# GLA's values as seven products of half sums, with the four GLA heads spread over three gated units

## The chip, the core and the metric

The kernel runs on one core of a Trainium2 chip. A core has a matrix engine (PE, TensorE; PEld is its weight load), VectorE (DVE), ScalarE (ACT), GpSimd (POOL), and SyncE (SP), whose queue issues most DMAs; POOL's queue issues others, among them DMAs that add to what lies at their destination. Each engine works off its own instructions in a fixed order and waits on semaphores. The metric is device time in microseconds; less is better.

## What is computed

One layer of a hybrid encoder: 512 tokens of width 2048, float32.

```python
mod = silu(c) @ w_cond + b_cond
shift, scale, gate = split(mod, 3)
h = rms_norm(x) * (1 + scale) + shift
aq, ak, av, ag, gq, gk, gv, gg, lr_f, lr_b = split(h @ w_in)
# attention, 16 heads x 64: three dilated windows merged by their denominators
a_out = att * silu(ag)
# GLA, 4 heads, dk 128, dv 256: gated linear attention, forward and backward
log_g = log_sigmoid(lr @ gate_up + bias) / 16
g_out = rms_norm(o_fwd + o_bwd) * gla_norm_gain * silu(gg)
y = concat(a_out, g_out) @ w_out
out = rms_norm(x + gate * y) * final_gain
```

The change concerns `gv = h @ w_in[:, 5120:6144]`: 512 x 2048 by 2048 x 1024.

## The kernel before

Every large product keeps its precision by splitting both operands: the high part is the value rounded to float32r (ACT copies it), the low part is the rest (DVE subtracts), and three matmuls make a product (high by high, low by high, high by low). A matmul has 128 rows of contraction and 512 columns. h lies split in SBUF (`h_hi`, `h_lo`, 16 tiles of 128 rows by 512 tokens). Weights come in groups of 512 KB: SP's queue loads them into one of 4 `raw` buffers (`fetch`), ACT and DVE split them into one of 3 `whi` and `wlo` buffers (`split_hi`, `split_lo`; L375 is the low half's line, L395 and L399 the high half's). Raw buffers also hold halves of the conditioning sums' weights.

PE's order is written by hand. After a first stage come *units* (`unit`), each a product with 512 columns of w_in: qk2, qk4, qk6 and gk with attention beside them, then gv0 and gv1 (GLA's values), ag0 and ag1 (attention's gate), gg0 and gg1 (GLA's gate). A unit has 8 groups of 24 matmuls. Side work is a list of (place, function), the place a fraction of the unit; what falls at 1 or later spills into the next unit. DVE, ACT, POOL and SP are ordered by a scheduler that follows the program and puts urgent items ahead, apart from what `keep_in_program_order` fixes.

- *GLA heads* (`gla_head`): two gates (z, then a chain on ACT and DVE with a scan, which ends in ki and qi), two `turn`s (three PE transposes of ki into kt), two `states` (kv and a chain DVE, POOL, ACT), `att`, two `outs` (go), `norm` (gn). GLA_AT gives their places; heads 0 to 3 stand in gv1, ag0, ag1 and gg0. The gates need the low-rank product plr, made in gv0.
- *Conditioning sums* (`cond_sum`, L269): 24 products of a row with 128 x 2048 weights, on DVE, whole (one load of 1 MB into an 8 KB buffer) or as two halves. SUMS_IN says how many a unit takes; the rest goes to gg1.
- *Output projection*: two pairs, each by Strassen's scheme on halves: products a to g in 28 steps of 12 matmuls, with the operands' sums of w_out (T1, T2, T3, U) made beforehand through DRAM by POOL's DMAs (`sum_begun` copies, `sum_ended` adds), and the sums of the left side (s57, s36, n6 and so on) on DVE at gg1's end and in the first steps. T3 is made in units qk6 to gv1 as a copy of T2 and an addition. `SUM_DMAS` says how many such DMAs a group of a unit issues.

## Time and profile before

| | |
|---|---|
| median of 3 runs | 926.52 us (926.39 to 926.55) |
| the profiled execution | 926.38 us, span 924.7 us |
| granted TensorE clock | 0.996 |
| units gv0 and gv1 | from 448.74 to 555.98 us |
| ag0, ag1, gg0 | to 718.38 us |
| gg1 | to 761.93 us |
| HBM | 200.5 MB read, 37.8 MB written |

A row of the groups' view has line, engine, operation, operands, count, busy time and mean duration, then the idle time before it and what ended that. In the windows, each stretch has its length and the busy time of each engine. In the timeline each row starts with its start and its duration. In the chain a row has its start and the time it covers.

### The profile page before, as it was taken

How to read it: one execution, taken by the hardware profiler on the slowest of the kernel's cores; microseconds unless marked ns; L12 is line 12 of the kernel's file. 1: busy time of each engine (PE TensorE's matmuls, PEld its weight loads, DVE VectorE, ACT ScalarE, POOL GpSimd, SP SyncE). 2: the span in 40 equal slices, each digit the busy share in tenths (PEclk: the TensorE clock that was granted, in tenths of full speed). 3: DMA queues.
4: the chain of work that ended last, by engine and by line, in shares of the span. 5: the costliest groups of instructions: out<-in, count | busy, mean ns of one | idle time of the engine just before them, and what ended most of it. 6: DMA issues, size and time to landing. Idle time of an engine off the chain costs nothing.

```text
span 924.7 us, 11717 instructions
## 1 busy us (share of the span) xinstructions
PE 913.2 (99%) x4273; PEld 756.4 (82%) x4273; DVE 674.1 (73%) x989; ACT 463.0 (50%) x743; POOL 134.5 (15%) x192
## 2 busy tenths in 40 slices
PE   8999999999999999999999999999999999999996
PEld 6888888888888888888878888888888888888885
DVE  7999899677776777778466658485585739678486
ACT  4543633555655655555414545373644439455455
POOL 7400000042152222222222210100000000000000
PEclk9999999999999999999999999999999999999998
DMA  9999787387599975696599855234243437756754
GB/s 339 412 413 414 266 308 267 111 266 275 176 223 268 255 243 182 175 252 174 208 366 330 233 134 187 112 114 138 92 138 113 157 139 237 285 197 225 278 189 181
DMA packets 51977, 209.75 MB, mean 227 GB/s; under 512 B 6888, under 2 KB 7440, under 8 KB 45520
## 3 DMA queue, kind: packets, MB, share of 16 engines
q1 hardware_dynamic: 43136, 170.58, 50.8%
q0 software_dynamic: 8352, 37.89, 16.5%
q8 instruction: 33, 0.54, 0.2%
q10 hardware_dynamic: 432, 0.55, 0.2%
q14 instruction: 24, 0.20, 0.1%
HBM read 200.52 MB, written 37.83 MB: 258 GB/s over the span
## 4 chain that ended last, share of the span: by engine, by line
PE 95%; DVE 2%; ACT 1%; DMA 1%; issue 0%; SPq 0%; DVEq 0%
PE op L1326 8%; PE ps_qk L168 5%; PE ps_qk L169 5%; PE ps_qk L170 5%; PE oq L1326 5%; PE o L720 3%; PE ps_gv L170 3%; PE ps_gv L169 3%; PE ps_ag L168 3%; PE ps_ag L170 3%; PE ps_gv L168 3%; PE ps_gg L169 3%; PE ps_gg L168 3%; PE ps_ag L169 3%; PE ps_gg L170 3%; PE stb L170 3%
## 5 line engine op out<-in xcount | busy, mean ns | idle before, releaser
L269 DVE CUSTOM_DVE_ANT_0 cb<-cb,sb,c_bcond 128x2048 f32<-128x2048 f32 (+1 forms) x32 | 74.0, 2312 | 5.0 <-DMA cb<-in_wm 4.9
L694 ACT ACTIVATE p<-p,st 128x512 f32<-128x512 f32 x64 | 46.0, 719 | 43.2 <-DVE st L691 38.8
L691 DVE CUSTOM_DVE_ANT_0 p<-s,g 128x512 f32<-128x512 f32 x64 | 43.4, 683 | 2.7 <-PE s L688 2.4
L269 DVE CUSTOM_DVE_ANT_0 sumg<-sumg,sb,c_bcond 128x2048 f32<-128x2048 f32 (+1 forms) x16 | 30.1, 1881 | 14.3 <-DMA sumg<-in_wg 14.3
L707 PEld LDWEIGHTS t<-c_ident,p 128*128 128x128 f32 x256 | 31.9, 141 | 8.4
L707 PE MATMUL t<-c_ident,p 128*128 128x128 f32 x256 | 38.3, 272 | 0.0
L660 POOL DMA_DIRECT2D ks<-ks x16 | 8.3, 519 | 201.4 <-DVE qs L651 168.9
L1243 POOL TENSOR_SCALAR x<-x,rn 128x512 f32<-128x512 f32 x1 | 1.3, 1253 | 219.6 <-ACT rn L1227 219.6
L696 DVE TENSOR_SCALAR p<-p,st 128x512 f32<-128x512 f32 x64 | 31.0, 485 | 1.8
L877 POOL TENSOR_SCALAR pair<-pair,sc 128x256 f32<-128x256 f32 x16 | 9.5, 593 | 156.4 <-DVE pair L874 145.7
L687 PE MATMUL s<-ks,qs 128*128 128x512 f32 x64 | 25.2, 393 | 0.0
L688 PE MATMUL s<-kl,qs 128*128 128x512 f32 x64 | 25.0, 390 | 0.0
L695 DVE RECIPROCAL st<-st 128x1 f32<-128x1 f32 x64 | 10.2, 160 | 19.4 <-ACT p L694 19.3
L884 ACT ACTIVATE sq<-pair,sc 128x256 f32<-128x256 f32 x24 | 12.2, 508 | 19.5 <-DVE pair L879 12.5
L291 POOL TENSOR_SCALAR lnm<-lnm,rel 16x207 f32<-16x207 f32 (+7 forms) x14 | 18.7, 1352 | 4.9 <-DMA lnm<-in_lnm 4.9
L269 DVE CUSTOM_DVE_ANT_0 sumv<-sumv,shb 128x1024 f32<-128x1024 f32 (+1 forms) x8 | 14.0, 1755 | 6.4 <-DMA sumv<-in_wv 6.4
L465 ACT ACTIVATE h_hi<-xt,shift 128x512 fp32r<-128x512 f32 x16 | 11.4, 718 | 11.3 <-DVE shift L269 11.3
L333 POOL DMA_DIRECT2D T<-in_w_o x24 | 17.0, 758 | 0.2 <-issue 0.2
L915 PE MATMUL go<-qi,sq 128*128 128x128 f32 x96 | 15.9, 275 | 0.0
L723 ACT ACTIVATE pair<-o 64x512 f32<-64x512 f32 x16 | 9.5, 596 | 11.8 <-PE o L720 11.4
L269 DVE CUSTOM_DVE_ANT_0 sumg<-sumg,sb,gate 128x1024 f32<-128x1024 f32 x7 | 9.1, 1298 | 7.5 <-DMA sumg<-in_wg 7.5
L687 PEld LDWEIGHTS s<-ks,qs 128*128 128x128 f32 x64 | 12.0, 187 | 2.7
(1689 smaller groups left out, 3169.3 us busy)
## 6 DMA issues: line engine op xcount, KB each, us to landing
cb<-in_wm SPq DMA_DIRECT2D x31, 1024.0 KB, 10.6
T<-in_w_o POOLq DMA_DIRECT2D x32, 512.0 KB, 8.4
raw_qk<-in_w_qk SPq DMA_DIRECT2D x24, 512.0 KB, 4.7
sumg<-in_wg SPq DMA_DIRECT2D x9, 1024.0 KB, 6.5
rawb<-in_w_sb SPq DMA_DIRECT2D x16, 512.0 KB, 6.7
U<-in_w_o POOLq DMA_DIRECT2D x16, 512.0 KB, 9.6
T<-T POOLq DMA_DIRECT2D x16, 512.0 KB, 5.3
raw_gv<-in_w_gv SPq DMA_DIRECT2D x16, 512.0 KB, 4.6
```

The costliest lines, as they stand in the source:

```text
L168: mm(ps, lh, rh, start=first, stop=False)
L169: mm(ps, ll, rh, start=False, stop=False)
L170: mm(ps, lh, rl, start=False, stop=last)
L269: return nc.vector.tensor_tensor_reduce(out=w, in0=w, in1=with_, op0=ALU.mult, op1=ALU.add, scale=1.0, scalar=init, accum_out=dst)
L687: mm(ps, qs[:, q], ks, start=True, stop=False)
L688: mm(ps, qs[:, q], kl, start=False, stop=True)
L691: nc.vector.tensor_tensor_reduce(out=t, in0=ps, in1=gt[h][:, P * i:P * i + 512], op0=ALU.add, op1=ALU.min, scale=1.0, scalar=3e38, accum_o ...
L694: act(t, t, AF.Exp, bias=st[:, 0:1], scale=-1.0, accum_out=st[:, 1:2])
L696: nc.vector.tensor_scalar(t, t, st[:, 2:3], None, op0=ALU.mult)
L707: nc.tensor.transpose(pk[:, kt * P:kt * P + P], t[:, kt * P:kt * P + P], ident)
L720: mm(po, vv[h // 4][:, kt, h % 4, :], parts[w][:, kt, :], start=kt == 0 and w == 0, stop=kt == 3 and w == 1)
L1326: mm(ps[:, c], l_, r_[:, c], start=first and z == 0, stop=last and z == 2, skip_group_check=not new)
```

## The change

GLA's values are no longer two units. The 512 tokens, the 2048 rows and the 1024 columns are halved, and seven products a to g, with operands that are sums of halves, take the place of eight; 28 steps of 12 matmuls in the order a, b, f (half), c, d, e, f (half), g.

- The sums of halves of w_in's columns (T1 and U) are made by POOL's DMAs in qk2 and qk4. T2 and T3 are added in place onto T1's memory while the products run (`sum_in_place`).
- The sums of halves of h are made by DVE in the attention units, eight operations per unit behind the scores (`h_sums_behind_scores`), stored to DRAM by POOL, loaded by SP step by step (`h_load`) and split (`h_split`).
- q of GLA leaves SBUF for DRAM in the meantime (`gqd`, `gq_back`).
- plr's 32 matmuls stand beside steps 2 to 17; the low-rank part follows.
- GLA_AT has a row for each head, counted in units from ag0 on: head 0's gates and turns stand in the last steps of the values (negative places), the rest of the four heads in ag0, ag1 and gg0, with a last piece in gg1.
- SUMS_IN: two sums in the values (their load whole, DVE's work in two parts), 5 in ag0, 4 in ag1, 4 in gg0, so 5 instead of 3 in gg1.
- The output projection's T3 is added in place onto T2's memory during steps c of each pair; its copies and early additions are gone, and the other sums of w_out stand later (`SUM_DMAS`).
- The gate's ACT operations are put ahead of others by the scheduler.

```diff
-GLA_AT = (0.01, 0.02, 0.33, 0.46, 0.46, 0.56, 0.63, 0.76, 0.76, 0.88)
-GLA_FIRST = 0.2
-SUMS_IN = {"qk6": 2, "gk": 2, "gv0": 8, "gv1": 2, "ag0": 3, "ag1": 2, "gg0": 2}
+GLA_AT = ((-0.45, -0.43, -0.12, -0.05, 0.03, 0.1, 0.18, 0.3, 0.3, 0.4),
+          (0.42, 0.45, 0.73, 0.8, 0.81, 0.88, 1.06, 1.17, 1.17, 1.29),
+          (1.32, 1.36, 1.67, 1.74, 1.75, 1.84, 1.9, 2.06, 2.06, 2.2),
+          (2.23, 2.27, 2.56, 2.63, 2.65, 2.75, 2.82, 2.92, 2.92, 3.08))
+SUMS_IN = {"qk6": 2, "gk": 2, "gv": 2, "ag0": 5, "ag1": 4, "gg0": 4}
...
+    groups += [("S", ("v", n, q)) for n, qs in (("a", range(4)), ("b", range(4)), ("f", (0, 1)), ("c", range(4)),
+                                               ("d", range(4)), ("e", range(4)), ("f", (2, 3)), ("g", range(4)))
+               for q in qs]
...
+    def sum_in_place(pair, name, q):
+        dsum[pair, name, q] = dsum[pair, SUMS[name][0], q]
+        sum_ended(pair, name, q)
...
-    SUM_DMAS = {"qk2": 2, "qk4": 2, "qk6": 1, "gk": 1, "gv0": 1, "gv1": 1}
+    SUM_DMAS = {"qk2": 2, "qk4": 2, "qk6": 1, "gk": 1, "ag0": 1, "ag1": 1, "gg0": 1}
...
+        return [whole(S7, k1, 0), whole(S5, k1, 1),
+                lambda: tt(slot(S7), slot(S7), slot(S5), op=ALU.subtract),
+                whole(N6, k2, 1),
+                lambda: tt(slot(S5), slot(N6), slot(S5), op=ALU.subtract),
+                lambda: stt(slot(N6), slot(S7), -1.0, slot(N6), op0=ALU.mult, op1=ALU.subtract),
+                whole(S3, k2, 0), last]
...
+    def v_product(z, t):
+        _, n, q = v_steps[z]
+        hi, lo = wts[gi["S", v_steps[z]]]
+        ps = vbank[V_BANK[n]][t]
+        new = n in "abf"
+        for kk in range(2):
+            lh, ll = v_left(z, kk, t)
+            c = slice(512 * kk, 512 * kk + 512)
+            first, last = new and q + kk == 0, q + kk == 4
+            for x, (l_, r_) in enumerate(((lh, hi[:, c]), (ll, hi[:, c]), (lh, lo[:, c]))):
+                mm(ps, l_, r_, start=first and x == 0, stop=last and x == 2, skip_group_check=not new)
...
+    side += [(3 + k, lambda k=k: lr_tick(k)) for k in range(KT)] + [(18.7, low_rank), (16, gq_back)]
+    side += [(2 + 24 * at, go) for at, go in some_sums("gv", "parts", 1.7)]
+    heads = [x for h in range(GH) for x in gla_head(h)]
+    side += [(28 + 16 * at, go) for at, go in heads if at < 0]
+    spill[:] = [x for x in heads if x[0] >= 0]
...
+        for ahead in (2, 3):
+            fetch(i + ahead)
+        if n in "bc":
+            sum_in_place("v", "T2" if n == "b" else "T3", q)
+        for y in range(z, z + 4):
+            h_load(y)
+        for y in (z, z + 1):
+            h_split(y)
...
-    ps = unit("gg0", False, gla_head(3) + some_sums("gg0"))
+    ps = unit("gg0", False, some_sums("gg0"))
...
+        if n == "c":
+            sum_in_place(pair, "T3", q)
```

How the instructions stand is decided by the scheduler, so three places are shown as the built programs have them. PE has 3876 rows before and 3828 after; the 48 rows that go are matmuls of the values.

First, the end of the values on DVE in the kernel after (ov.. are the values' weight splits by product and step, gv the results, z, g, b, bm, ki and qi the gates of head 0, ag00l the first split of the next unit):

```order
L383 TENSOR_TENSOR ovg1l<-raw_ovg_4705,ovg1h 128x1024
L860 TENSOR_TENSOR ki_4657<-ki_4657,gkt 128x512
L861 TENSOR_TENSOR qi_4656<-qi_4656,gqb 128x512
L837 TENSOR_SCALAR g_4680<-z_4674,c_gbias 128x512
L1165 TENSOR_TENSOR gv_4707<-vr_4285,vkeepa_4172 128x512
L1165 TENSOR_TENSOR gv_4707<-vr_4286,vkeepa_4174 128x512
L838 TENSOR_TENSOR g_4680<-g_4680,e_4676 128x512
L383 TENSOR_TENSOR ovg2l<-raw_ovg_4724,ovg2h 128x1024
L845 SCALAR_TENSOR_TENSOR b_4683<-rst,g_4680 128x512
L383 TENSOR_TENSOR ovg3l<-raw_ovg_4744,ovg3h 128x1024
L854 TENSOR_TENSOR bm_4688<-b_4683 128x512
L383 TENSOR_TENSOR ag00l<-raw_ag_4763,ag00h 128x1024
```

The next row is the second ki. On PE that ki's transposes (kt) stand in the middle of the last step, g3:

```order
L1149 MATMUL vp_4064<-ovg3h,h_lo_130 128x512
L1149 MATMUL vp_4064<-ovg3l,h_hi_126 128x512
L870 MATMUL kt_4817<-c_ident,ki_4692 128x128 x3
L1149 MATMUL vp_4065<-ovg3h,h_hi_126 128x512
L1149 MATMUL vp_4065<-ovg3h,h_lo_130 128x512
```

In before the first head's gates stood beside gv1, with nothing but weight splits and sums between them; now they stand among splits that a step of 2.72 us wants and among the products' results.

Second, the middle of the values on SP's queue in the kernel after (T1v is the memory in which T1, then T2, then T3 lie; hrb and hrc are loads of the h sums for b and c, gqb GLA's q, ovf, ovc and ovd weights):

```order
L359 DMA raw_ovf_4203<-in_w_gv 128x1024
L1123 DMA hrb_4179<-hs_1504 128x512
L359 DMA raw_ovf_4228<-in_w_gv 128x1024
L359 DMA raw_ovc_4254<-T1v_1548 128x1024
L1123 DMA hrc_4257<-hs_1501 128x512
L359 DMA raw_ovc_4281<-T1v_1550 128x1024
L359 DMA raw_ovc_4307<-T1v_1584 128x1024
L359 DMA raw_ovc_4333<-T1v_1586 128x1024
L1123 DMA hrc_4283<-hs_1502 128x512
L1123 DMA hrc_4309<-hs_1503 128x512
L1123 DMA hrc_4336<-hs_1504 128x512
```

Each load of c reads what POOL's addition of T2 has written; three of c's four h sums are queued behind the last of them.

Third, POOL's queue at the output projection in the kernel after (T_4836 and the others are the memories of T2, which the steps c load):

```order
L351 TENSOR_SCALAR seen<-gg10h 1x1
L336 DMA T_4836<-in_w_o 128x1024
L336 DMA T_4900<-in_w_o 128x1024
L336 DMA T_4950<-in_w_o 128x1024
L336 DMA T_5013<-in_w_o 128x1024
L336 DMA T_5105<-in_w_o 128x1024
L336 DMA T_5141<-in_w_o 128x1024
L336 DMA T_5183<-in_w_o 128x1024
L336 DMA T_5237<-in_w_o 128x1024
```

In before POOL's queue issued nothing here; the same additions stood beside gv1, behind copies into memory of their own.

More of the change, by code (lines that the diff above doesn't have):

```diff
@@ L1051, in block_kernel, with lr_tick @@
-    gla["lr"] = lrr
-    upr = RAW("upr", [2, 512])
-    nc.sync.dma_start(upr, a["up"])
-    gla["up"] = gp.tile([P, 2, 512], F32R, tag="g", name="ups")
-    act(gla["up"], upr, AF.Copy)
-    tt(gla["up"][64:128], upr[64:128], gla["up"][64:128].bitcast(F32), op=ALU.subtract)
-    gla["rst"] = T2("rst")
-    nc.scalar.dma_start(gla["rst"], a["rst"])
-    ps = unit("gv1", True, gla_head(0) + some_sums("gv1", "whole", 1.7, 0.5))
-    gla["v1"] = B8("gv1", [4, 512])
-    for i in range(4):
-        act(gla["v1"][:, i, :], ps[i], AF.Copy)
+    def lr_tick(k):
+        if k == 0:
+            gla["plr"] = PA("plr")
+        plr = gla["plr"]
+        w = lrs[:, k, :, :].rearrange("p a b -> p (a b)")
+        mm(plr[:64], w, h_hi[:, k, :], start=k == 0, stop=False)
+        mm(plr[:64], w, h_lo[:, k, :], start=False, stop=k == KT - 1)
```

178 lines of the change are left out of this document (134 added, 44 removed).

## The prediction

> **What bounds the kernel now.** I read the shares of busy time on the page first, then its chain of work, then the answer on who waited for whom, filtered to PE (all its rows are here).
>
> ```profile
> PE 913.2 (99%) x4273; PEld 756.4 (82%) x4273; DVE 674.1 (73%) x989; ACT 463.0 (50%) x743; POOL 134.5 (15%) x192
> ...
> PE 95%; DVE 2%; ACT 1%; DMA 1%; issue 0%; SPq 0%; DVEq 0%
> ...
> PE hot L211 <- DVE idle L197: 1.5, 1, 1.5
> PE sta L168 <- ACT h_hi L434: 0.4, 1, 0.4
> PE sta L169 <- DVE h_lo L437: 0.4, 1, 0.4
> PE pc L261 <- POOL selb L192: 0.2, 1, 0.2
> ```
>
> TensorE is 95% of the chain, and its only four waits (2.5 us) lie in the opening. From there to the end it never stands still, so whatever it is spared comes straight off the span, until another engine is late. How far the others are from that is seen by stage, in the busy time of each engine per window: the unit qk4 (250.98), gv0 (448.74), gv1 (501.89), the start of the output products (761.93), and their steps c and d (784.20).
>
> ```profile
> 250.98:316.96 65.98, 65.98 (x322) 54.44 (x321) 47.48 (x101) 36.50 (x70) 21.76 (x32) 1.00 1.01 248
> 448.74:501.89 53.15, 53.15 (x234) 41.85 (x233) 32.72 (x31) 14.69 (x18) 13.02 (x16) 1.00 0.85 326
> 501.89:555.98 54.09, 54.09 (x271) 45.89 (x270) 29.26 (x35) 24.58 (x42) 11.85 (x18) 1.00 0.75 198
> 761.93:784.20 22.27, 22.19 (x98) 18.03 (x97) 22.20 (x27) 21.38 (x29) 0.00 (x0) 1.00 0.68 228
> 784.20:805.98 21.78, 21.78 (x97) 17.99 (x96) 13.03 (x13) 10.06 (x12) 0.00 (x0) 1.00 0.83 293
> ```
>
> After the length stand PE, its weight loads, DVE, ACT, POOL, then the granted clock (1.00) and the DMA share. In gv0 and gv1 DVE works 62 of 107 us: there is room. In the first steps of the output products DVE is full (22.20 of 22.27) and PE still lost 0.08 us: splits for products of halves can keep up at one step per 2.72 us.
>
> **The change part by part.** *TensorE.* gv0 and gv1 were 2 x 192 matmuls of 512 columns. The seven products are 28 steps of 12, thus 336. The 32 matmuls of plr, the heads and everything else keep their number, so 48 go.
>
> ```profile
> 587.87 1.78 PE att L894 x16
> 595.11 4.46 PE go L915 x40
> 773.49 10.88 PE oq L1326 x48
> ```
>
> The last row of this piece of the chain is 48 such matmuls: 10.88 us, 0.2267 each. That is the whole gain; **926.38 - 10.88 = 915.50 us** if nothing else is late. (926.38 is the profiled execution, 1.7 over its span of 924.7; the three runs shown have a median of 926.52.) The copies of T3 that are dropped, and the sums moved between units, are off the chain; I give them nothing.
>
> *DVE and ACT in the values.* The price of a step, from the timeline of ag0 (DVE) and of the output products (ACT); what counts is from one start to the next:
>
> ```profile
> 567.40 1.22 DVE L830 TENSOR_TENSOR_SCAN b<-rst,g 128x512 f32<-128x512 f32 x1
> 568.54 1.20 DVE L375 TENSOR_TENSOR ag03l<-raw_ag,ag03h 128x1024 fp32r<-128x1024 f32 x1
> 569.65 0.68 DVE L839 TENSOR_TENSOR bm<-b 128x512 f32<-128x512 f32 x1
> 570.26 1.22 DVE L375 TENSOR_TENSOR ag04l<-raw_ag,ag04h 128x1024 fp32r<-128x1024 f32 x1
> ...
> 770.57 1.06 ACT L395 ACTIVATE o0b1h<-raw_o0b 128x1024 fp32r<-128x1024 f32 x1
> 771.53 0.61 ACT L1082 ACTIVATE s360h<-s 128x512 fp32r<-128x512 f32 x1
> ```
>
> A scan is 1.14, a weight split 1.11 on DVE and 0.96 on ACT, a 512-wide operation 0.61 on DVE and at most 0.61 on ACT. The stage lasts 336 x 0.2267 + 32 x 0.2267 = 83.4 us, with the first gates and transposes some 84.6. DVE: 28 splits 31.1, 16 splits of h sums 9.8, four half sums 4.8, head 0's gates 2 x (1.14 + 5 x 0.61) = 8.4, some 17 more operations (attention's end, low rank, six results) 10.4: 64.5 us, 76%. ACT: 26.9 + 9.8 and some 18 for the rest, 65%. On average both fit; the cost lies in places.
>
> *The end of the values.* I follow DVE's row of work by the order given with the change, from the last product d (0 us; e takes to 11.3, f to 16.8, g0 to g3 to 19.5, 22.2, 25.3 and 28.3). A step's split can't start before the step three back has left its buffer. ovf3l ends at 10.7; then come g, two results, the first scan, ovg0l at 15.6, bm, ovg1l at 17.4, ki, qi, g, two results, ovg2l at 22.2 (wanted by 22.6), the scan, ovg3l at 24.5, bm, ag00l, and only then head 0's second ki, at 26.9. Its three transposes stand amid step g3, at 26.6: **+0.4 us** with the turn-round. Ends: 0 and 2 (every row at its full length instead of start to start).
>
> *Head 0 in ag0.* Five whole sums use one slot in turn. The period of such a slot, DMA and sum, is seen in before's ag0, and so is what the chain wants:
>
> ```profile
> 554.86 2.34 DVE L269 CUSTOM_DVE_ANT_0 sumg<-sumg,sb,c_bcond 128x2048 f32<-128x2048 f32 x1
> ...
> 562.09 2.35 DVE L269 CUSTOM_DVE_ANT_0 sumg<-sumg,sb,c_bcond 128x2048 f32<-128x2048 f32 x1
> ...
> 591.45 0.69 DVE L901 SCALAR_TENSOR_TENSOR at<-c_ident,at 128x512 f32<-128x512 f32 x1
> ```
>
> 7.2 us a sum, of which 4.9 the load. On the same clock the first sum starts at 27.5, so the third can't start before 27.5 + 2 x 7.2 = 41.9; with two chained head operations queued between them I get 42.0. Behind it stand copy_predicated and the operation on at: done at 45.6. PE has by then done ag00, kv twice, ag01, att (1.78) and half of ag02, from 28.7 to 45.4, and wants go: **+0.3 us**, ends 0 and 3 (a load of 1 MB that takes 7.9 us, the median row below). In before at was ready at 592.1 and go came at 595.1: 3 us of cover, which the third sum uses up.
>
> *The start and the middle of the values: DMA.* The window from 255 to 335 us holds the accumulating sums of the weights; its DMA rows, after two rows of the whole page:
>
> ```profile
> raw_qk<-in_w_qk SPq DMA_DIRECT2D x24, 512.0 KB, 4.7
> ...
> sumv<-in_wv SPq DMA_DIRECT2D x4, 1024.0 KB, 7.9
> ...
> q0 software_dynamic: 3360, 11.54, 68.9%
> q1 hardware_dynamic: 2330, 8.65, 29.1%
> ...
> T<-in_w_o POOLq DMA_DIRECT2D x8, 512.0 KB, 13.8
> raw_qk<-in_w_qk SPq DMA_DIRECT2D x8, 512.0 KB, 8.3
> U<-in_w_o POOLq DMA_DIRECT2D x8, 512.0 KB, 15.3
> ```
>
> 29.1% of 80 us for 8.65 MB is 1.41 us of all engines per 512 KB load; 68.9% for 11.54 MB is 2.5 us per sum. The values' stage wants 28 weight loads, 16 half loads, q (two) and two sums of sumv (four): 42 x 1.41 = 59.2, and nine accumulating sums, 22.5: 81.7 of 84.6 us. It fits, barely, with about five steps loaded ahead. Two places:
>
> Start: ovb0l stands in DVE's queue behind the first half of the second sumv, whose load waits for the slot of the first (free at 4.7 us in the stage). b0 wants ovb0l at 14.1; with a half sum (1.2) and the split before it, the load must take under 7.0. The row says 7.9, ag0's period 4.9: **+0.5 us**, ends 0 and 0.9. Middle: T2 is made in place as b's loads land; the fourth sum starts near 16 us. c3's load waits for it on SP, and the h sums of c1, c2 and c3 are queued behind c3's load. c1 starts at 35.8; its h sum, half a load, must land (some 5.6, between 4.7 and 8.3) and be split (1.2), so T2's fourth sum must land by 29, 13 us after its start. Rows: 13.8 in the crowd; 15.3 at worst: **+0.5 us**, ends 0 and 2.3.
>
> *T3 in place.* The sum that stood early now runs beside the loads of c and d of the output products. There the tightest load in before is o0d2:
>
> ```profile
> 771.54 0.32 SPq L351 DMA_DIRECT2D raw_o0c<-T  x1
> 775.64 0.32 SPq L351 DMA_DIRECT2D raw_o0c<-T  x1
> ...
> raw_o0c<-T SPq DMA_DIRECT2D x4, 512.0 KB, 5.9
> ...
> 787.21 0.33 SPq L351 DMA_DIRECT2D raw_o0d<-in_w_o  x1
> ...
> 794.91 1.06 ACT L395 ACTIVATE o0d2h<-raw_o0d 128x1024 fp32r<-128x1024 f32 x1 [4.21 <-DMA raw_o0d<-in_w_o]
> ...
> 796.00 1.23 DVE L375 TENSOR_TENSOR o0d2l<-raw_o0d,o0d2h 128x1024 fp32r<-128x1024 f32 x1 [4.05 <-ACT o0d2h L395]
> ...
> L1326 PE MATMUL oq<-o0d2l,s361h x4: 389/389/389, 798.3 to 800.3; 128*128 128x512 f32 x4
> ```
>
> ACT waited 4.21 us for it, DVE was done at 797.2, PE wanted it at 798.3: 1.1 us to spare. T3's sums for c0 and c1 (5.0 us of all engines) start as those loads land, 5.9 us after their issue, near 777 and 782. Until 794.9 the windows leave 17% of 11 us and 32% of 6 idle, some 3.8, of which I count 2.8, since it is scattered. The load comes 2.2 later: **+1.1 us**, ends 0 and 4. The later loads have over 2 us to spare. What company costs is seen above: beside POOL's sums a load landed after 8.3 us, not 4.7. The Trainium skill, "DMA: Bandwidth & Descriptors", section "Queues, rings and completion order", says that each DMA engine takes the queues that have work in turn, packet by packet; by that rule the idle share would not help the load, which is the second rival below, and the trace's 8.3 agrees with it in kind.
>
> *h sums in attention.* Eight operations per unit, 4.9 us on a DVE that works 47.5 of 66. Each is queued behind a score's last operation, so it delays the next by 0.61. The later scores' tight place in before:
>
> ```profile
> 369.12 0.48 DVE L696 TENSOR_SCALAR p<-p,st 128x512 f32<-128x512 f32 x1
> ...
> 371.19 0.49 PE L707 MATMUL t<-c_ident,p 128*128 128x128 f32 x3
> ```
>
> 1.6 us of cover: nothing, ends 0 and 1 (two in a row at a tight place).
>
> Sum: 915.5 + 0.5 + 0.5 + 0.4 + 0.3 + 1.1 = **918.3 us**.
>
> **The rivals.** *No stall at all*: each of the five terms has 0 as an end, and PE has held beside a DVE at 100%. Time 915.5. Against it: five places at once with under 1 us of cover. *T3's sums and the loads take turns*: the idle share does not help, o0d2 meets all 5.0 us instead of 2.2, and PE waits 3.9 there instead of 1.1: 921.1. For it: the 8.3 us beside sums. Against it: the loads of x stand in the same stretch and already cost o0d2 7.7 us, and PE had 1.1 left. *DMA becomes the bound of the values*: counted as the page does, the stage moves 51 x 0.524 = 26.7 MB; at qk4's 248 GB/s (share 1.01) that is 108 us. Less some 13 loaded ahead it is 95 against 84.6: 10 us given back, 925.5. Against it: two thirds of qk4's traffic were sums, of the values' a quarter. *Slower*: T2's four sums are served one after another, each in 13.8 us; the fourth lands at 53 instead of 29, SP stands at c3's load meanwhile with the h sums behind it, and PE waits some 24 us: 940. It decides for slower than before from 10.9 us a sum, when the fourth lands at 42. Against it: sixteen sums and four copies were issued within those 80 us, so they overlap at some 4 to 5 us each. That the matmuls are not saved can't be: the order of PE has 48 fewer.
>
> **How the numbers follow.** Forecast 918.3 (916.5 to 920.5 by itself): 0.45. No stall: 0.27. T3 in turns: 0.11. DMA's bound: 0.11. Serial T2: 0.06. A measurement here tells 0.2% (1.9 us) from nothing, so faster is below 924.6: 0.45 + 0.27 + 0.11 and 0.05 of DMA's bound, 0.88; the same 0.06, slower 0.06. The range from 915.2 to 925.5 leaves out serial T2 and half of the DMA case.
>
> **What would show it.** PE's busy matmuls 48 fewer; new rows among PE's waits, at kt and go of head 0, at the products of b0 and c1, and at o0d2, none over 4 us; o0d2's load longer than the 7.7 us from 787.2 to 794.9; the values' stage 83 to 86 us long with a DMA share near 0.95. The forecast is wrong if PE waits in the attention units, or in heads 1 to 3, where I count nothing, or if the granted clock leaves 1.00.

## The result, and the profile after

The changed kernel takes **939.0 us** (median of 4 runs, 937.3 to 939.8); the kernel before 926.5 in the same comparison. The ratio is 1.0133 with a 95% interval of 1.0115 to 1.0150: slower by 1.3%, 12.5 us, where 8 us less were forecast, and far above the range. The profiled execution took 938.63 us with a span of 936.9, against 926.38 and 924.7 before.

The page of the changed kernel first: busy time, two rows of the DMA queues, and the chain that ended last.

```profile
PE 911.5 (97%) x4225; PEld 748.9 (80%) x4225; DVE 718.1 (77%) x1071; ACT 482.9 (52%) x771; POOL 144.1 (15%) x221
...
q1 hardware_dynamic: 48176, 182.11, 53.8%
q0 software_dynamic: 11376, 51.52, 23.2%
...
PE 74%; DMA 13%; DVE 7%; issue 2%; ACT 2%; SPq 0%; DVEq 0%; ACTq 0%
```

The 48 matmuls are gone (4273 to 4225). But PE was 95% of the chain and is 74%; DMA has 13%. Who PE waited for in the whole program (us in total, times, longest; two groups of 0.2 us that follow are left out):

```profile
PE gn L945 <- DVE gsl L943: 3.6, 2, 2.8
PE vq L1149 <- ACT hpb3h L1129: 2.5, 1, 2.5
PE go L930 <- DVE at L916: 2.3, 1, 2.3
PE oq L1469 <- ACT keep1b L1425: 1.9, 1, 1.9
PE hot L211 <- DVE idle L197: 1.5, 1, 1.5
PE vp L1149 <- ACT hpc1h L1129: 1.2, 1, 1.2
PE vp L1149 <- DVE ovc2l L383: 0.5, 1, 0.5
PE oq L1469 <- DVE o0d2l L383: 0.5, 1, 0.5
PE vq L1149 <- DVE hpb1l L1130: 0.4, 1, 0.4
PE oq L1469 <- ACT o0d2h L403: 0.4, 1, 0.4
PE kt L870 <- DVE ki L860: 0.3, 1, 0.3
```

Behind each of the long waits stands a load: hpb3h and hpc1h split sums of h, gsl and at are queued on DVE behind sums of the gate's weights, and keep1b on ACT behind a split of o1c1 (the wait hot lies in the opening and was there before). ACT's rows for the last of these:

```profile
872.97 1.06 ACT L403 ACTIVATE o1c1h<-raw_o1c 128x1024 fp32r<-128x1024 f32 x1 [5.10 <-DMA raw_o1c<-T]
873.93 0.58 ACT L1425 ACTIVATE keep1b<-oq 128x512 f32<-128x512 f32 x1
```

The same is seen by stretch; in the columns, after the length, PE's busy time, its weight loads, DVE, ACT, POOL, the granted clock, the DMA share and GB/s. The rows are the whole values, their products b with the first half of f, and c, the unit ag1, and c with d of the output for pair 0 and pair 1.

```profile
449.09:545.32 96.23, 91.14 (x385) 70.16 (x384) 64.27 (x76) 52.13 (x75) 7.30 (x9) 0.98 0.90 279
462.74:487.56 24.82, 21.80 (x85) 15.94 (x84) 11.24 (x13) 9.88 (x13) 4.07 (x5) 0.93 1.00 292
487.56:503.72 16.16, 14.08 (x58) 9.77 (x57) 7.42 (x8) 7.30 (x10) 0.81 (x1) 1.00 1.02 300
602.49:664.72 62.23, 56.91 (x288) 47.44 (x286) 39.79 (x57) 29.34 (x49) 11.08 (x19) 1.00 0.74 195
790.74:814.02 23.28, 22.40 (x97) 17.79 (x96) 12.78 (x13) 9.92 (x11) 1.91 (x3) 1.00 1.02 336
868.42:893.96 25.54, 23.65 (x97) 19.08 (x96) 10.22 (x9) 9.96 (x12) 2.42 (x3) 0.93 0.95 303
```

In these stretches of the values and the output the DMA share is 0.95 to 1.02; in ag1 it is 0.74. The two clocks of 0.93 are stretches at half clock right behind a wait, seen closer in the first of these two windows:

```profile
470.00:480.00 10.00, 7.44 (x25) 5.21 (x24) 3.05 (x3) 3.23 (x4) 0.81 (x1) 0.83 1.01 302
480.00:490.00 10.00, 10.00 (x45) 7.90 (x44) 3.05 (x3) 3.12 (x4) 2.47 (x3) 1.00 1.00 227
```

A clock of 0.83 over 10 us is 3.4 us at half, so 1.7 us lost behind the wait of 2.5.

**The balance.** As a measure of each stage without waits I take the shortest that it had in any run below; a stage runs from its first product to the next stage's. The four gated units 223.2 us against 215.95 (57.16 + 56.14 + 58.61 + 44.04; 205.95 before, so the change moves 10.0 of head work into them); the values 96.25 against 86.4 (the 107.2 of gv0 and gv1, less 10.88 and these 10.0); output 168.5 against 162.7 before; attention 0.35. That is 7.2 + 9.9 + 5.7 + 0.35 = 23.2 us of new time, of which two half-clock stretches make 3.4. Less 10.88 it is 12.3, and the spans differ by 12.2. That this closes is no check, because the values' 86.4 is worked out from the kernel before; the shortest lengths of the values' own products in the runs below add up to 86.9, which would put 9.3 in the place of the 9.9.

The values' stretch from 448 to 505 us, its DMA rows (packets, MB, share of 16 engines; then x, KB each, median us to landing), what SyncE's queue issued there, and ACT's use of hrb3:

```profile
q1 hardware_dynamic: 3857, 12.61, 59.7%
q0 software_dynamic: 1152, 4.19, 38.5%
...
hrc<-hs SPq DMA_DIRECT2D x4, 256.0 KB, 14.4
...
456.03 0.51 SPq L1113 DMA_DIRECT2D gqb<-gqd  x1
461.90 0.33 SPq L359 DMA_DIRECT2D raw_ovf<-in_w_gv  x1
462.34 0.37 SPq L1123 DMA_DIRECT2D hrb<-hs  x1
...
468.89 10.76 SPq L359 DMA_DIRECT2D raw_ovc<-T1v  x3
479.71 1.54 SPq L1123 DMA_DIRECT2D hrc<-hs  x3
...
475.34 0.63 ACT L1129 ACTIVATE hpb3h<-hrb 128x512 fp32r<-128x512 f32 x1 [7.73 <-DMA hrb<-hs]
```

59.7% of 57 us for 12.61 MB is 1.41 us of all engines for 512 KB, as predicted; 38.5% for eight sums is 2.74 each (predicted 2.5). Together that is 98%. hrb3 was issued at 462.34 and used at 475.34, 13.0 us for 256 KB.

### The profile page after: what moved, and what is told of

It reads as the page before. It is cut to its first block, busy times and chain, and to the rows that moved or that the text cites. A ratio compares the mean times of both kernels' runs of the same rounds, so it can differ in the third digit from the quotient of the medians.

```text
span 936.9 us, 11887 instructions
## 1 busy us (share of the span) xinstructions
PE 911.5 (97%) x4225; PEld 748.9 (80%) x4225; DVE 718.1 (77%) x1071; ACT 482.9 (52%) x771; POOL 144.1 (15%) x221
## 3 DMA queue, kind: packets, MB, share of 16 engines
q0 software_dynamic: 11376, 51.52, 23.2%
## 4 chain that ended last, share of the span: by engine, by line
PE 74%; DMA 13%; DVE 7%; issue 2%; ACT 2%; SPq 0%; DVEq 0%; ACTq 0%
PE op L1469 6%; DMA sumg<-in_wg 6%; PE ps_qk L168 5%; PE ps_qk L169 5%; PE ps_qk L170 5%; PE stb L170 3%; PE stb L168 3%; PE stb L169 3%; PE o L728 3%; PE sta L169 3%; PE vp L1149 3%; PE sta L170 3%; PE sta L168 3%; PE t L715 3%; PE oq L1469 3%; PE ps_gg L168 3%
## 5 line engine op out<-in xcount | busy, mean ns | idle before, releaser
L702 ACT ACTIVATE p<-p,st 128x512 f32<-128x512 f32 x64 | 46.0, 719 | 24.2 <-DVE st L699 22.3
L269 DVE CUSTOM_DVE_ANT_0 sumg<-sumg,sb,c_bcond 128x1024 f32<-128x1024 f32 (+1 forms) x16 | 23.7, 1483 | 19.4 <-DMA sumg<-in_wg 19.4
L269 DVE CUSTOM_DVE_ANT_0 sumg<-sumg,sb,gate 128x1024 f32<-128x1024 f32 x13 | 16.7, 1282 | 17.3 <-DMA sumg<-in_wg 17.3
L899 ACT ACTIVATE sq<-pair,sc 128x256 f32<-128x256 f32 x24 | 12.2, 507 | 27.9 <-DVE pair L889 16.9
L703 DVE RECIPROCAL st<-st 128x1 f32<-128x1 f32 x64 | 10.2, 159 | 12.6 <-ACT p L702 12.5
L473 ACT ACTIVATE h_hi<-xt,shift 128x512 fp32r<-128x512 f32 x16 | 11.4, 719 | 11.3 <-DVE shift L269 11.3
L731 ACT ACTIVATE pair<-o 64x512 f32<-64x512 f32 x16 | 9.5, 595 | 14.9 <-PE o L728 14.8
L336 POOL DMA_DIRECT2D T1v<-in_w_gv x12 | 9.4, 783 | 47.4 <-DMA raw_ovb<-T1v 28.9
L269 DVE CUSTOM_DVE_ANT_0 sumv<-sumv,shb 128x1024 f32<-128x1024 f32 (+1 forms) x8 | 11.9, 1488 | 5.0 <-DMA sumv<-in_wv 5.0
L932 ACT ACTIVATE gsq<-go 128x512 f32<-128x512 f32 x8 | 4.8, 597 | 21.1 <-PE go L930 21.1
```

The lines of the kernel that those rows point to most:

```text
L269: return nc.vector.tensor_tensor_reduce(out=w, in0=w, in1=with_, op0=ALU.mult, op1=ALU.add, scale=1.0, scalar=init, accum_out=dst)
L336: return nc.gpsimd.dma_start(dsum[pair, name, q], quadrant(pair, SUMS[name][1], q), accum_op=ALU.add, max_dma_last_dim=4096)
L702: act(t, t, AF.Exp, bias=st[:, 0:1], scale=-1.0, accum_out=st[:, 1:2])
```

## The experiments

Theory after the traces: **DMAs that only had to be done some time (T3's sums, gqb, T2's sums, sums of the gate's weights) stand beside or ahead of loads that are wanted soon.** Rivals: order alone (a load issued late on SyncE's queue), bytes alone (the stretch is full whatever the order), the sums' work itself. Lengths of stages in us; medians of all runs of a kernel; the kernel before had medians of 926.4 to 926.7 beside them. Stage lengths are of one profiled execution each, worked out from the starts of each stage's first product in the trace.

| kernel | values start | b + f | c | e | g | ag1 | gg0 | gg1 | a/b 0 | c/d 0 | e-g 0 | c/d 1 | e to end | median |
|---|---|---|---|---|---|---|---|---|---|---|---|---|---|---|
| changed | 449.1 | 24.8 | 16.2 | 17.0 | 11.8 | 62.2 | 59.7 | 44.0 | 22.3 | 23.3 | 32.6 | 25.5 | 43.0 | 939.0 |
| e1 | 449.3 | 24.8 | 15.6 | 16.8 | 11.6 | 62.7 | 58.6 | 44.0 | 22.3 | 24.0 | 32.6 | 23.7 | 43.0 | 936.2 |
| e2 | 449.2 | 25.6 | 15.5 | 16.8 | 11.6 | 60.6 | 59.9 | 44.0 | 22.3 | 25.7 | 32.7 | 22.2 | 43.0 | 937.3 |
| e8 | 449.5 | 26.2 | 15.1 | 16.8 | 11.6 | 62.0 | 60.0 | 44.0 | 22.3 | 23.2 | 32.7 | 23.6 | 43.1 | 938.7 |
| e3 | 449.1 | 24.8 | 16.5 | 16.8 | 11.6 | 57.4 | 58.6 | 46.2 | 26.4 | 23.1 | 32.6 | 23.1 | 43.0 | 935.8 |
| e4 | 449.2 | 24.8 | 16.5 | 16.8 | 11.6 | 56.1 | 60.0 | 49.6 | 25.9 | 23.3 | 32.6 | 23.2 | 43.3 | 942.2 |
| e7 | 449.2 | 25.2 | 16.1 | 16.9 | 11.7 | 56.2 | 65.3 | 44.1 | 22.2 | 24.3 | 32.6 | 22.8 | 43.0 | 936.5 |
| e5 | 449.0 | 26.1 | 13.6 | 16.8 | 11.6 | 63.7 | 58.7 | 44.0 | 22.3 | 23.8 | 32.6 | 23.5 | 42.3 | 936.5 |
| e6 | 449.3 | 20.2 | 16.8 | 16.8 | 11.6 | 63.3 | 59.0 | 44.0 | 22.2 | 23.9 | 32.6 | 23.8 | 43.0 | 933.6 |
| e9 | 449.3 | 25.0 | 12.8 | 16.8 | 14.2 | 62.6 | 59.9 | 44.0 | 22.2 | 23.1 | 32.6 | 22.1 | 43.0 | 938.8 |
| e10 | 449.1 | 23.7 | 19.3 | 16.8 | 11.6 | 65.0 | 58.8 | 44.0 | 22.3 | 21.8 | 37.3 | 21.8 | 45.2 | 941.2 |
| e11 | 449.2 | 24.8 | 16.6 | 16.8 | 11.6 | 61.5 | 58.6 | 44.0 | 22.2 | 23.9 | 32.6 | 23.4 | 42.3 | 936.2 |
| e12 | 449.2 | 28.8 | 12.8 | 16.8 | 11.7 | 59.4 | 58.6 | 44.0 | 22.3 | 23.3 | 32.9 | 22.8 | 42.1 | 932.1 |
| e13 | 459.3 | 23.2 | 16.7 | 16.8 | 11.6 | 56.1 | 58.6 | 44.0 | 22.3 | 24.3 | 32.6 | 25.8 | 43.0 | 940.1 |
| e14 | 449.0 | 21.2 | 12.8 | 20.9 | 11.8 | 65.0 | 59.3 | 44.0 | 22.3 | 21.8 | 32.6 | 21.8 | 44.4 | 934.2 |
| e15 | 460.8 | 24.7 | 12.8 | 20.8 | 11.8 | 56.1 | 58.6 | 44.0 | 22.3 | 21.8 | 33.4 | 21.8 | 45.7 | 940.9 |
| e16 | 448.6 | 19.2 | 14.8 | 16.8 | 11.6 | 62.4 | 58.7 | 44.0 | 22.3 | 21.8 | 32.8 | 21.8 | 43.6 | 928.6 |
| e17 | 448.8 | 19.2 | 12.8 | 20.5 | 11.8 | 62.5 | 59.5 | 44.0 | 22.2 | 21.8 | 33.3 | 21.8 | 44.8 | 930.4 |
| e18 | 449.1 | 20.4 | 17.3 | 16.8 | 11.7 | 61.7 | 58.9 | 44.0 | 22.2 | 21.9 | 33.9 | 21.8 | 44.9 | 930.8 |

The values' products a and d, ag0 and a/b of pair 1 are not in the table; they vary by at most 0.7 us over all rows. Where PE waits, a stage differs from execution to execution and some waits draw half-clock stretches that cost 1.7, 3.4 or 5.1 us; a median that differs by 2 or 3 us says little here, the stages say more. The expected totals were missed almost throughout, and always to the slow side: only e1 (935.5 expected, 936.2 measured) and e6 (933.5 and 933.6) came within 2 us, and e1's edit moved nothing, as shown next. What the texts below are worth is read from the stages that they name.

### T3's sums moved in the program only (e1, e2, e8)

```diff
-        if n in "bc":
+        if n in "be":            # e1, values
-        if n == "c":
+        if n == "e":             # e2, output; e8: n == "ce"[pair]
```

> The in-place T3 sums of the values are issued during product e in place of c (8 steps later); nothing else moves. Theory (DMA bound in b and c, and T3's four sums of about 2.5 us each are part of what fills it): the PE waits of product c (about 3.3 us) go, those of b stay, because T3's sums start only at 479 us, behind b's waits: about 935.5 us. Rival 1 (the loads of h's sums and of the weights alone fill the queues; T3 is small beside them): c's waits stay, 938 to 939 us. Rival 2 (T3 is then late for product g): a new wait ahead of g, 939 to 945 us.

> The in-place T3 sums of the output stage are issued during product e in place of c, in both pairs. Theory (the sums run beside the doubled loads of c and d and make d late): the waits in c/d of both pairs go, with the half-clock stretch that follows the wait of pair 1: 23.28 and 25.54 us of c/d back to about 21.8, so about 933.5 us. Rival (the second loads of x and the doubled weight loads alone make d late): c/d stays within 0.7 us in each pair, 938 to 939 us.

> The output's in-place T3 sums stay in product c for pair 0 and go to product e for pair 1. Theory (pair 1's wait at o1d0 and the half-clock stretch behind it come from those sums, and in pair 0 the loads of x were put ahead of o0c2 when T3 was moved): c/d of pair 1 from 25.5 to about 22.0 us, c/d of pair 0 as before at 23.3 us, the whole about 935 us. Rival (pair 0's 25.7 us in the run with both pairs moved comes from another cause): pair 0 at 25 us or more here too, and 937 us.

These three tested nothing. POOL's rows of the changed kernel, and then of e1:

```profile
478.94 0.81 POOL L336 DMA_DIRECT2D T1v<-in_w_gv  x1 [11.46 <-DMA raw_ovc<-T1v]
```

```profile
478.56 0.81 POOL L336 DMA_DIRECT2D T1v<-in_w_gv  x1 [11.23 <-DMA raw_ovc<-T1v]
```

POOL's queue had nothing else ahead, so it issued each sum as soon as c's load had left the place in DRAM, wherever the program writes it; in e2 and e8 too the output's sums start at the same places (781.6 and 783.6 us, 782.8 in the changed kernel). In all three traces the rows of each engine stand in the order of the changed kernel. So these are three more executions of it, and a first measure of how its stages scatter: c 15.1 to 16.2, ag1 60.6 to 62.7, c/d of pair 0 23.2 to 25.7. (e10 below, whose edit leaves the times of the values' sums as they were, goes further: c 19.3 and ag1 65.0, each with a half-clock stretch of 6.8 us.) e2's pair 1 (22.2) looked like a success of the theory and was scatter.

### T3's sums held on POOL (e9, e10)

```diff
+        if behind is not None: tc.keep_in_program_order(nc.gpsimd.tensor_scalar(seen, behind.bitcast(F32)[0:1, 0:1], ...))
+        tc.keep_in_program_order(sum_ended(pair, name, q))
...
+        if n in "be": sum_in_place("v", ..., None if n == "b" else wts[i][0])    # e9
+        if n == "e":  sum_in_place(pair, "T3", q, wts[i][0])                     # e10
```

> In the first try T3's sums were only written later in the program; POOL's queue had nothing ahead of them and issued them at the same times (478.6 to 487.6 us). Here each is held on POOL behind a 1x1 instruction that reads product e's weights, so they start at about 517 us. Theory (bandwidth: four sums of about 2.5 us fill a part of c's DMA time): c from 16.2 (15.1 to 16.8 over the runs so far) to under 14.5 us, b unchanged at 24.8 to 26 us, about 936 us. Rival (order: c waits because hrc1 to hrc3 are issued only when SyncE has got rid of raw_ovc2 and raw_ovc3): c stays above 15 us, 938 to 939 us. If T3 comes too late for g: a wait at ovg, and the stage e to g longer than 28.4 us.

> The same hold for the output stage: T3's sums start in product e of each pair, from about 814 and 894 us. Theory: c/d of pair 0 from 23.8 us (mean of the runs so far, 23.1 to 25.7) to about 22 us, of pair 1 from 23.2 us (22.2 to 23.8 without a half-clock stretch) to about 21.9 us, so 3 to 5 us less: about 935 us. Rival (the loads of x and fgain and the doubled weight loads make d late): both stay at 23 to 24 us, 938 to 939 us. If T3 comes too late for g: e to a of pair 0 longer than 32.7 us, or a wait at o1g.

Now the sums do start later; e9's rows of POOL and its windows of b and c, to be held against those of the changed kernel above:

```profile
507.87 1.18 POOL L341 TENSOR_SCALAR seen<-ove0h 1x1 f32<-1x1 f32 x1 [40.31 <-ACT ove0h L403]
509.00 0.59 POOL L336 DMA_DIRECT2D T1v<-in_w_gv  x1
```

```profile
462.95:487.90 24.95, 21.83 (x85) 15.99 (x84) 12.55 (x15) 11.56 (x16) 1.61 (x2) 0.93 0.98 321
487.91:500.74 12.83, 12.83 (x58) 10.09 (x57) 6.11 (x6) 5.88 (x8) 0.00 (x0) 1.00 0.64 214
```

PE does not wait in c at all (12.83 of 12.83 us; DMA share 0.64 where it was 1.02), and b is as before. In e10 the waits of c/d are gone in both pairs:

```profile
794.24:816.02 21.78, 21.78 (x97) 17.99 (x96) 13.03 (x13) 10.06 (x12) 3.23 (x4) 1.00 0.84 296
816.02:853.32 37.30, 34.55 (x146) 28.12 (x144) 25.46 (x32) 15.40 (x21) 3.15 (x5) 0.95 0.78 226
875.08:896.84 21.76, 21.76 (x98) 18.02 (x96) 10.24 (x9) 9.98 (x12) 3.24 (x4) 1.00 0.73 239
```

So **T3's sums make the waits of c and of the output's c/d, in both pairs**; the loads of x and the doubled weight loads, which were the rival for c/d, do not make them alone. Nor does the late issue of hrc1 to hrc3, the rival for c: e9 issued them at 480.2 to 481.2 us, as late as the changed kernel (479.7 to 480.7), and they were there within 5.6 us in place of 11.7 to 17.1. But the middle row shows where it went: g's first load now waits for T3's first sum, which lands at 821.5 us, and lands itself at 829.4 (37.3 us for 32.6, and 2.2 us more at the end); in e9 g takes 14.2 for 11.6. There is no gain in the medians.

### The loads of b: gqb later (e6), h's sums on ScalarE's queue (e5)

```diff
-        nc.sync.dma_start(gla["q"], dstore)
+        tc.keep_in_program_order(nc.sync.dma_start(gla["q"], dstore))            # e6
-            nc.sync.dma_start(h_raw[z]..., h_sums[q][:, SLOT[n]])
+            nc.scalar.dma_start(h_raw[z]..., h_sums[q][:, SLOT[n]])              # e5
```

> The load of gqb (1 MB from DRAM, issued at 456.0 us) is pinned behind the loads that the program has traced before it, which puts it among product e's loads. Theory (bandwidth and first come first served in SyncE's queue: gqb's about 3 us stand ahead of ovf0 and hrb3): hrb3 lands about 3 us earlier, the wait at b3 shrinks from 2.9 us to under 0.5 us and the half-clock stretch behind it (1.7 us) goes, c's late loads follow: b to f and c from 41.0 to 34 to 37 us, the whole about 933.5 us. Rival (hrb3 waits for its buffer, not for gqb): b3 still waits over 2 us, 938 to 939 us; a load too late for head 0 would show as a wait at kt.

> The sixteen loads of the sums of h (hrb to hre, 256 KB each) are issued on ScalarE's queue in place of SyncE's; nothing else changes, no byte more or less. Theory (order: on SyncE's queue they stand behind weight loads that wait for a buffer and behind the 1 MB of gqb and sumv; hrc1 was issued only at 479.7 us): the waits at b3 (2.9 us, and the half-clock stretch behind it) and at c1 go, b to f and c together from 41.0 to 33 or 34 us, the whole about 932 us. Rival (bandwidth: the DMA share of 448 to 505 us is 0.99, so what h's sums gain the weights lose): the waits move to the weights ovb, ovf and ovc, the two stages stay at 39 to 41 us, the whole 937 to 939 us.

e6 does what was expected for b: hrb3 is used 3.8 us earlier, the wait and the half clock are gone, b + f 24.8 to 20.2. Its windows of b + f and c, and ACT's row:

```profile
462.99:483.23 20.24, 19.80 (x85) 15.05 (x84) 11.10 (x13) 9.89 (x13) 4.07 (x5) 1.00 1.00 294
483.23:500.05 16.82, 13.96 (x57) 9.77 (x56) 6.87 (x8) 6.80 (x9) 0.81 (x1) 1.00 1.04 296
...
471.53 0.63 ACT L1129 ACTIVATE hpb3h<-hrb 128x512 fp32r<-128x512 f32 x1 [3.68 <-DMA hrb<-hs]
```

c did not follow: its waits stay, as T3's sums do. The whole went to 933.6, as expected (933.5), though not part by part. In e5 c loses its waits (13.6), but not in the way that its theory has it: ScalarE's queue issued hrc1 to hrc3 at 482.1 to 485.1 us, later than SyncE's did in the changed kernel (479.7 to 480.7). They landed after 9.4 to 11.4 us in place of 11.7 to 17.1, and c began 1.2 us later; why they took less is not shown. b does not get better, for something else is late now:

```profile
465.71 1.23 DVE L269 CUSTOM_DVE_ANT_0 sumv<-sumv,shb 128x1024 f32<-128x1024 f32 x1 [4.39 <-DMA sumv<-in_wv]
```

DVE stood 4.4 us for the 1 MB of sumv with hpb1l queued behind it, and PE 3.8 us for hpb1l.

### The heads: fewer sums (e3), T2 elsewhere (e4, e7, e13), sums loaded whole (e11)

```diff
-SUMS_IN = {..., "ag0": 5, "ag1": 4, "gg0": 4}      -> gg1 has 5
+SUMS_IN = {..., "ag0": 5, "ag1": 2, "gg0": 4}                    # e3: gg1 has 7
-SUM_DMAS = {"qk2": 2, "qk4": 2, "qk6": 1, "gk": 1, "ag0": 1, "ag1": 1, "gg0": 1}
+    ... "gk": 1, "gg0": 1, "gg1": 1}                             # e4
+    ... "gk": 1, "ag0": 1, "gg0": 1}                             # e7
+    "qk2": 2, "qk4": 3, "qk6": 2, "gk": 1}                       # e13
-    some_sums(f"ag{j}", *(("halves",) if j else ("whole", 1.0)))
+    some_sums(f"ag{j}", "whole", 1.0)                            # e11
```

> Two of ag1's four sums of the gate (four loads of 512 KB, four sums on VectorE) are left to gg1. Theory (VectorE stands in order on those loads, so at and gsl of the heads come late): the waits at go and gn in ag1 (2.7 and 3.1 us) go, ag1 from 62.2 to about 57 us; gg1 has room, 44 to 45 us: about 933 us. Rival (the waits come from the copies and sums of w_o's T2 that run on POOL's queue in ag0 and ag1): the waits shrink by under a third, 937 to 939 us.

> The sixteen DMAs that make w_o's T2 move from ag0 and ag1 to gg0 and gg1; the sums on VectorE stay. Theory (the number of sums in ag1 makes the heads late): the waits at go and gn in ag1 shrink by under a third, 937 to 939 us, or more where T2 then runs into gg0. Rival (T2's traffic makes the loads of the sums land late): go and gn in ag1 lose most of their 5.8 us, about 933 us.

> The eight copies and sums of w_o's T2 that ag1 issues go to gg0 (ag0 keeps its eight, gg0 has eight, gg1 none); the sums on VectorE stay 5, 4, 4 and 5. Theory (in ag1 it is the meeting of four sums' loads with T2's DMAs that makes the loads late; taking out either is enough, as the two runs with fewer sums and with T2 later showed with 57.4 and 56.1 us for ag1): ag1 62.2 to about 56.5 us, gg0 59 to 60 us, gg1 44 us as before, since T2 is out of it: about 933 us. Rival (ag1's gain was only moved, and comes back wherever T2 meets sums): gg0 62 us or more, the whole 937 us or more.

> ag1's four sums are loaded whole (1 MB each into an 8 KB buffer, one sum ahead), as ag0's are, in place of halves through the weights' buffers half a sum ahead; bytes, VectorE's work and T2's DMAs stay. Theory (the loads are merely issued too near to their use for what a load takes beside accumulating DMAs, 5.0 us median and 8.7 at most in ag1): the waits at go and gn go, ag1 62.2 to 57 us: about 933 us. Rival (ag1 has too many bytes and the wait comes wherever the loads are issued): ag1 61 us or more, 938 us.

> The copies and sums that make w_o's T2 go from ag0 and ag1 into the attention units before them (24, 16 and 8 of POOL's DMAs in qk4, qk6 and gk in place of 16, 8 and 8); nothing else. Theory (accumulating DMAs beside loads that are issued about a microsecond or two ahead of their use are what makes ag1 long): ag1 62 to 56.2 us with all four sums left in it, gg0 58.6, gg1 44.0 and no new wait, since the attention units' loads are issued long ahead: about 932 us. Rival (the DMAs are too many wherever they go): PE waits in qk4 to gk, or the values, which then meet the last of T2's sums, longer than their 96 us by as much as ag1 is shorter: 937 us or more.

e4 ends ag1's waits (56.1 us) and e3 all but 1.2 us of them (57.4), so neither theory of that round was the whole one: it takes the sums' loads **and** T2's DMAs. The eight copies come first, then the eight accumulating sums, and only the second half costs: copies stood in ag0 in the changed kernel (57.2 us, as in e13 without any) and in gg0 in e4 (60.0, where four runs with no T2 there have 59.7 to 60.0), sums in ag1 (62.2), in gg1 in e4 (49.6 for 44.0) and in gg0 in e7 (65.3 for 58.6, with a wait of 3.8 us and half clock behind it). Each time DVE stands on a load of a sum (7.1 us at most in e4's gg1, 4.2 in e7's gg0, with the heads' work queued behind it); DVE's waits in ag1, of the changed kernel and of e13:

```profile
DVE sumg L269 <- DMA sumg<-in_wg: 16.7, 8, 5.2
```

```profile
DVE sumg L269 <- DMA sumg<-in_wg: 2.2, 4, 1.3
```

With the same four sums in ag1 and no T2 there, the waits fall from 16.7 to 2.2 us, and e13 has all four units at their shortest: 7.2 us less. e13 then gives 10.2 back ahead of the values. Its window of qk4 (65.98 us in the changed kernel) and its PE waits, of which the first lies in qk4 and the second in qk6:

```profile
250.89:322.38 71.49, 67.83 (x322) 55.52 (x321) 52.09 (x109) 36.95 (x70) 25.39 (x42) 0.98 0.97 285
...
PE s L695 <- DVE st L699: 3.7, 1, 3.7
PE s L695 <- DMA ks<-ks: 2.7, 1, 2.7
```

T2's DMAs push T1's and U's forward, so that 24 of these stand in qk4 in place of 16, and T2's own follow in qk6 and gk. At the first wait DVE stood 4.7 us on a load (g); at the second PE wanted a copy of k (ks), which POOL's queue issued behind T1's sums at 320.8 us and which landed 13 us later. e11, ag1's loads one sum ahead, takes DVE's waits for them from 16.7 to 7.7 us, and yet PE waits 2.2 us at gn and 1.2 for a silu (sga) on ACT (61.5): an earlier issue alone is no cure. e3's two sums more in gg1 make the gate late, 2.2 and 4.2 us in gg1 and behind it.

### Together (e12, e14, e15), and fewer bytes in the values (e16, e17, e18)

```diff
# e12: e5 + e6 + e11
# e14: e6, and T3 held earlier:
+        if n in "bd": sum_in_place("v", ..., None if n == "b" else wts[i][0])
+        if (n, q) == ("d", 3):
+            for z in range(4): sum_in_place(pair, "T3", z, wts[i][0])
# e15: e14 + e13
# e16: e6, the output's T3 as in e14, and
+SUMS_IN = {"qk6": 3, "gk": 3, "gv": 0, "ag0": 7, "ag1": 2, "gg0": 4}
# e17: e16 and the values' T3 as in e14
# e18: e16 with "qk6": 2, "gk": 2, "gv": 2
```

In the texts that follow, e15's "two kernels before" are e13 and e14; the kernel that e17 starts from and e18's "first kernel" are e16.

> Three edits together: gqb's load among product e's, h's loads on ScalarE's queue, ag1's sums whole; T3's sums as in the changed kernel. Theory: b to f 20.2 or less (as with gqb later alone) and c 13.6 (as with ScalarE's queue alone), 33.8 us for 41.0; ag1 57 for 62.2; less about 12.4 us: 926 to 927 us, as before, with the output's 3 to 4 us left. Rival (bandwidth of the values: what one edit frees the other takes): b to f and c together 36 us or more, 929 us or more.

> Three things held back, no byte more or less: gqb's load among product e's, the values' T3 sums behind product d's weights (one a step), the output's T3 sums behind the last weights of product d. Theory: b to f 20.2 us, c 12.8, no wait at g (with the hold to e it was 14.2 us for 11.6), c/d of the output 21.8 in both pairs, and with T3 five to ten microseconds earlier than with the hold to e no wait at g there either (e to a of pair 0 32.7, tail 21.2): with ag1 at 61 to 63 us about 925 us. Rival (held sums are late for g however they are held, or meet d's or e's loads): ovd, ove or ovg longer by 2 us or more, e to a of pair 0 over 34 us, the whole 929 us or more.

> The two kernels before together. Theory (four places where accumulating DMAs or an early bulk load meet loads that are needed soon make the whole loss): the values 88 us, ag0 to gg1 216 us, output 163 to 164 us: 918 to 920 us, faster than the kernel before by 0.7 to 0.9%, which is the sum of the prediction without its stalls. Rival (something of the Strassen values costs besides): 923 us or more.

> Four edits: gqb later; the output's T3 behind the last weights of product d; no conditional sums in the values (3, 3, 0 in qk6, gk and the values in place of 2, 2, 2); seven sums in ag0, two in ag1 (5 and 4 before). T2's DMAs and the values' T3 stay. Theory (DMA volume beside near loads): the values lose 2 MB (gqb moved too: 3 MB) out of b's stretch, so b to f 19.1 to 20.2 us and c 14 to 16.8; ag0 57 to 58, ag1 57.4 as with two sums there, gg0 58.6, gg1 44.0 with its five sums and no late gate; output c/d 21.8 in both pairs, tail at most 22.7: about 923 to 925 us. Rival (the third sum in qk6 and gk makes the attention units wait, as T2's DMAs did): start of the values after 450 us by as much, 927 us or more.

> As the kernel before with the values' T3 sums held behind product d's weights. Theory: c 12.8 us in place of 14 to 16.8, and e, which took 20.9 us with gqb and T3 together beside its loads, 16.8 to 19, since 2 MB of sums are gone ahead of it: 921 to 923 us, faster than the kernel before by 0.4 to 0.6%. Rival (the stage is bound by its bytes, whatever the order): c's gain comes back in e, 923 to 926 us.

> As the first kernel here, but with the sums of before in qk6, gk and the values (2, 2, 2). Theory: b to f 20.2 and c 16.8 us, as with gqb later alone, 1 to 3 us over the first kernel: about 925.5 us, which is the time before within 0.2%. Rival (the values' sums do not matter): the same time as the first within 0.7 us.

e12: c has no waits, but b loses 6.5 us at one place (hpb1l behind sumv again), b to c take 41.6 us and the whole 932.1: the rival's side. e14: c, and c/d of both pairs, are free, g nearly so, but e takes 20.9 us for 16.8, and the whole 934.2 where 925 was expected. ACT's row and the window of e:

```profile
513.00 0.63 ACT L1129 ACTIVATE hpe1h<-hre 128x512 fp32r<-128x512 f32 x1 [4.86 <-DMA hre<-hs]
...
509.49:530.39 20.90, 18.18 (x75) 13.58 (x74) 16.73 (x21) 13.24 (x20) 0.00 (x0) 1.00 0.85 294
```

This load (hre1) was issued at 499.37, behind gqb's megabyte (496.63) and beside T3's sums (492.1 to 501.8), and landed after 13.5 us; in e6, with gqb but not T3 there, it took 8.7. e15 adds e13 and with it its loss: 940.9 where 918 to 920 was expected. So **in none of the orders tried did all of the values' waits end: without those of b, c kept its own (e6), and without those of c new ones came in e (e14) or g (e9)**. That no order does it is not shown: e6 with e9's hold, for one, was not run. A full DMA alone is no wait either: d of e14 ran at a share of 1.01 and e of e9 at 1.00, both with PE at work throughout.

e16 takes 2 MB out of the values (no sums of the conditioning there): b + f falls to 19.2, with PE never waiting, and c to 14.8. e18, the same with these two sums, has 20.4 and 17.3, which is 3.7 us more; but e16's profiled execution is the fastest of its twelve and e18's the slowest of its eight, and their medians differ by 2.2. e17 shows the move again: c 14.8 to 12.8, e 16.8 to 20.5, the whole 930.4 where 921 to 923 was expected. ag1 with two sums did not keep its 57.4 where ag0 has seven: PE waited there 2.4 us for a silu of ag0 (sga) on ACT, and 1.4 for gsh.

e16 is the fastest, 928.6 us (925.6 to 932.3 over 12 runs), ratio to before 1.0024 (1.0011 to 1.0038): 10 us better than the changed kernel, and still slower than before by a hair. No version was faster than before. None had the heads of e13 with the attention units undisturbed; e13's 215.95 us of heads with e16's other stages would take 6.3 us from e16, some 919 from its profiled (and fastest) execution or 922 from its median, but no run shows that the two can be had together.

## Why the prediction was wrong

**Matmuls.** Right: 48 fewer, 10.88 us. **Start of the values** (0.5): nothing, no wait at b0. **End of the values** (0.4): right, 0.4 us in e and g together, 0.3 of it at kt as said. **Head 0 at go** (0.3): nothing; ag0 is 57.2 us with and without T2's copies.

**Middle of the values** (0.5): this step failed. It was 9 us (b + f 24.8 against 19.2, c 16.2 against 12.8). The sum "81.7 of 84.6 us. It fits, barely" had nearly the right prices (1.41 and 2.5 us predicted, 1.41 and 2.74 measured) and was read as a yes. Two things made it a no. The load is not even: in the 57 us in which T2's and T3's eight sums, gqb and sumv come together the share is 98%, with 0.8 behind it. And what a load takes to land there was mis-sized: the h sum of c1 was given 5.6 us and took 11.7, that of b3 took 13.0 and was not considered. T2's fourth sum, in which the prediction sought the danger, landed 29.1 us into the stage, by when it had to land; gqb's megabyte ahead of hrb3 (e6) and T3's sums beside hrc (e9) made the waits. "DMA becomes the bound of the values" was among the rivals with the price of 10 us and a chance of 0.11, and the price came out (9.9), in part by luck: the stage moved 26.9 MB, as counted, but at 279 GB/s and not 248, and the 13 us taken off for loads made ahead were not saved. What spoke against it, that only a quarter of the values' traffic is sums, was no argument, since plain loads fill the rest. The stage, for which 83 to 86 us with a share near 0.95 were named, took 96.2 at 0.90.

**Heads 1 to 3** (nothing): failed, 7.2 us. The only sentence that covers the sums on VectorE and T2's DMAs in these units gives them nothing ("the sums moved between units, are off the chain"). Off the chain they were; but beside them a half sum's load took 5.0 us (median) and 8.7 at most, and 3.5 and 5.0 in e13 without them, and DVE, which works in order, held at and gsl behind it. The last sentence named the place: the forecast is wrong "if PE waits in the attention units, or in heads 1 to 3, where I count nothing".

**T3 in place** (1.1): right in mechanism and, at o0d2 of pair 0, in size: 1.5 us (10.0 us from o0d2's issue at 793.75 to its split at 803.8, 7.7 before). Pair 1 was waved through with "over 2 us to spare" and lost 3.8, of which 1.7 at half clock: o1c1's load, issued at 859.92 beside T3's first sum (859.84), landed after 12.9 us, and ACT stood on it for 5.1 with keep1b behind. The rival by which T3's sums and the loads take turns gave o0d2 3.9 us. The row lies near the forecast's 1.1. That rival's rule (the Trainium skill, "DMA: Bandwidth & Descriptors", section "Queues, rings and completion order": queues with work are served in turn, packet by packet) is not refuted by it, since the scatter of c/d in pair 0 over the runs reaches 25.7 us, as much as it asks.

**The clock.** Assumed at 1.00; two of the longer waits drew a half-clock stretch behind them, which cost 3.4 us of the 23.2 in the profiled execution.

Open: whether the accumulating DMAs cost more than their engine time says because they are taken in turn with the loads, or only because 2.74 us each fill what was left; no run doubles or halves their packets. In ag1 the share was only 0.74, so there a full DMA is not the whole account. Also whether T2 can be made where neither heads nor attention wait.

## What to carry to other kernels

Work that is off the chain still takes its share of a resource that the chain needs: before DMAs are moved or put beside a stage, add up the stage by stretches of some 50 us with the price of each kind of DMA. Where the sum comes near 100%, don't take it for a fit, nor for a wait as such (qk4 in the kernel before ran at a share of 1.01 and PE never stood): look for the loads in it that are wanted within 10 to 15 us of their issue, which is what they took here (13.0 and 14.4). A DMA that need not be early must be held (behind an instruction on its queue that reads something late), since its place in the program alone does not make it late; and a hold has an end as well, here g's loads. A load that an in-order engine stands on, such as DVE's sums, turns every late byte into a wait of all that is queued behind.
